# The first head's weights loaded and split ahead of the last modulation columns, the first group's features scaled as they are split, and weights in memory by tile

## The chip, the cores and the metric

The kernel runs on one core of one Trainium2 chip. The metric is the time of one execution on the device in microseconds (us), start to end; the median of several runs is used. The engines are PE (TensorE: matrix products and transposes), DVE (VectorE) and ACT (ScalarE) for the elementwise work, POOL (GpSimd) and SP (SyncE, which here only issues DMA transfers). Each engine runs its own instruction list in order and waits on semaphores for the others.

## The reference

One block of a diffusion transformer over x (2048 rows of 1024), with a context of 256 rows and a conditioning vector c. The modulation vectors come from c by a product with w_mod (1024 x 6144, six parts of 1024); the context has its own from c_ctx. Rows are normalised, scaled and shifted by two of the parts, and multiplied by w_in (1024 x 4608) for the queries, values, gates and decays of eight heads (four with learned decay, four retention heads), which run over the sequence in both directions. Then come an output product and a feed-forward part with a short convolution, w_up (1024 x 5632) and w_down.

```python
mod_x = (jax.nn.silu(c) @ w_mod[layer] + b_mod[layer])[:, None, :]
mod_c = jax.nn.silu(c_ctx) @ w_mod[layer] + b_mod[layer]
sh1, sc1, g1, sh2, sc2, g2 = jnp.split(mod_x, 6, axis=-1)
...
hx = _rmsnorm(x, norm1_g[layer]) * (1.0 + sc1) + sh1
hc = _rmsnorm(ctx, norm1_g[layer]) * (1.0 + csc1) + csh1
feats_x = _mixer_features(hx, w_in[layer], lb, (rows, cols))   # hx @ w_in, split by head
...
mix_x, _ = _bidir_mix(feats_x, ctx_states, log_gamma, ...)
x = x + g1 * (mix_x @ w_out[layer])
hx2 = _rmsnorm(x, norm2_g[layer]) * (1.0 + sc2) + sh2
x = x + g2 * _conv_ffn(hx2, w_up[layer], conv_w[layer], conv_b[layer], w_down[layer])
...
return _rmsnorm(x, final_g)
```

## The kernel before

**Tiling.** x is worked on in 4 groups of 512 rows (numbers 3, 2, 1, 0 at the start), the context as one group of 256. Large products use float16 pairs: a 32-bit tile v times a scale is kept as its rounded 16-bit value and the 16-bit rest, and a product takes three matmuls (lines 101, 102, 103). Seven products of blocks replace eight (a fast 2 x 2 scheme), so that both features and weights are kept as seven block combinations. "Splitting" means making these pairs: ACT writes the rounded value (`w[m][:, 0]`, `hx[..., 0]`), DVE the rest (`w[m][:, 1]`, `hx[..., 1]`), and DVE forms the sums and differences of blocks between.

**The start of the kernel,** which the change rewrites, consists of these chains:

- *Modulation* (`mod_loads`, `mod_first`, `mod_rows`). w_mod is loaded in column blocks of 512, named j4 = 2, 3 (the scale sc1), 0, 1 (the shift sh1), four tiles `wm` of 0.5 MB each. PE multiplies them with `silb` (silu of c) into `mod_ps`, 8 matmuls a column block (line 288); ACT copies the result to `modrow` (L254), four small matmuls turn it into columns (`modt_ps`, L259) and DVE adds the bias: `modT` (L262).
- *First rows.* The rows of group 3 (`x3`, in the buffers hc_145 to hc_151 and x_190) are loaded, squared and summed on ACT (L393), the reciprocal root comes from POOL, and ACT (L402) and DVE (L404) scale the rows.
- *First head's weights* (`head_weights(0)`). `items0` is a list of pairs (load, compute): w_z (two tiles `raw` of 0.5 MB), three further steps of its split, w_q (one tile), w_vg (two tiles, value and gate), three further steps. A compute step squares the raw tile on ACT (L738), sums over the partitions on PE (`allsum`, L124), takes a power of two as scale on DVE by five small operations (L112 to L116: `p2t`, `p2i`, `p2s`), then splits by `pair_blocks` (L691 on ACT, L692 on DVE; L748 and L749 for w_q) with the block sums on DVE (L536 to L545).
- *The feature scale* (`modulation`). From `modu` (gain times 1 + sc1) and `modT` a bound of all features is taken: `modj`, `modq`, a matmul that lays 128 partitions into a `row` (L138), a maximum (`allmax`, L140 and L142), the power of two s (`p2s`, L112 to L116), its inverse `dqx` (L366), and A = modu x s, B = modT x s (L368, L369).
- *First features* (`first_blocks`). For each pair of 128-columns kk and kk + 4, PE transposes the rows (`tp`, L411), ACT (L450) or DVE (L448) forms `ftmp` = tp x A + B, ACT casts (L429) and DVE subtracts (L430) into `hx`; afterwards eight block sums (L433, marked so in the profile) and their pairs follow. With `early=1` the two ftmp of the first column pair and its unit are formed with modu and modT as soon as these are known, and multiplied by s by DVE afterwards (L452).
- *First products.* hx times w_z (`p`), then w_q (`pa`), w_vg, with the gates (`FG`, `ct`, `cb`) between them on ACT and DVE; then the rows of group 2 (`x2`) are squared and normalised, and so on for all heads and groups.

**What sets the order.** The Python code only gives program order and buffers. `tile.TileContext(nc, schedule_with_timeline_sim=True)` makes the instruction order of each engine by a planner that simulates the program. So a small move in the code can move many rows. All loads shown go through one queue, SP's, in order. Weight tiles wait in buffers by tag ("wr" has two, "hx" seven); w_mod's first two column blocks lie in "hx", the raw tiles of w_vg in K1 and Q1.

**In memory** w_in, w_up and w_mod are kept as in the reference, rows of 4608, 5632 and 6144 numbers. A `raw` tile of 128 columns (`src[:, :, c:c + P]`) is thus read in pieces of 512 bytes, a `wm` tile in pieces of 2048 bytes.

Of the kernel before, what the change touches and what calls it, by code (L numbers as in the profile page):

```python
# [54 lines left out]
class Kern:  # L55
# [208 lines left out]
    def mod_loads(self):  # L264

        nc = self.nc
        wsrc = self.I["w_mod"][0].rearrange("(k p) n -> p k n", p=P)
        self.wm = []
        for j4, places in ((2, ("hx",) * 4), (3, ("hx",) * 4), (0, KEPT[:4]), (1, ("FG", "KTt", "ou0", "ou1"))):
            for k, tag in zip(range(0, KT, 2), places):  # L270
                w = self.slot_tile([P, 2, 512], F32, tag, "wm")
                nc.sync.dma_start(w, wsrc[:, k:k + 2, 512 * j4:512 * j4 + 512])
                self.wm += [(j4, k + i, w[:, i]) for i in range(2)]
            if j4 == 3:
                place = [h.rearrange("p k a t -> p (k a t)").bitcast(F32) for h in self.hc]
                place.append(self.slot_tile([P, G], F32, "qs", "x3"))
                self.x3 = self.load_rows(NG - 1, place)
            if j4 in (3, 1):
                self.items0[0 if j4 == 3 else 4][0]()

    def mod_first(self):

        nc = self.nc
        for j4, k, w in self.wm:
            if k == 0:
                ps = self.ps("sc", [P, 512], "mod_ps")
            q = k % 4 * B
            nc.tensor.matmul(ps[q:q + B], self.silb[:, k], w, start=k < 4, stop=k >= 4, skip_group_check=True)
            if k == KT - 1:
                if j4 == 2:  # L290
                    self.small_vectors()
                self.mod_rows(ps, 2, j4)

    def mod_later(self, j4):

        nc = self.nc
        wsrc = self.I["w_mod"][0].rearrange("(k p) n -> p k n", p=P)
        st = {}

        def item(k0):  # L300
            def load():

                st[k0] = w = [self.slot_tile([P, 512], F32, "q", "wm") for _ in range(2)]
                for kk in range(2):
                    nc.sync.dma_start(w[kk], wsrc[:, k0 + kk, 512 * j4:512 * j4 + 512])
# [108 lines left out]
    def first_blocks(self, g, xn, places, bank, early=0):  # L414
# [10 lines left out]
        def pair(m, u, v):  # L425
# [3 lines left out]
            cast = nc.scalar.copy(o[:, :, 0], v)  # L429
            self.tail = nc.vector.tensor_tensor(o[:, :, 1], v, o[:, :, 0], ALU.subtract), cast  # L430
# [4 lines left out]
        b = []  # L435
        for k0 in (0, 2):
            f = [places[k0 + r]() for r in range(2)]
            units = [(slice(k0, k0 + 2), f)] if len(f[0]) == len(f[1]) == 1 else [(slice(k0 + i, k0 + i + 1), []) for i in range(2)]
            for i in range(2):
                k = k0 + i  # L440
                at = [(v[0][:, i] if len(v) == 1 else v[i])[:, :2 * n] for v in f]
                for r in range(2):
                    kk = k + 4 * r
                    tp = self.transposed(xn, kk, bank)
                    A, B, s = self.plain if k < early else self.mod1
                    A, B = (v[:, which, kk:kk + 1] for v in (A, B))
                    if r and g in (None, NG - 1):
                        nc.vector.tensor_scalar(at[r], tp, A, B, ALU.mult, ALU.add)  # L448
                    else:
                        nc.scalar.activation(at[r], tp, AF.Identity, bias=B, scale=A)  # L450
                    if k < early:
                        nc.vector.tensor_scalar(at[r], at[r], s, None, ALU.mult)  # L452
                if len(units) == 2 or i:
# [255 lines left out]
    def head_weights(self, h):  # L709
# [317 lines left out]
    def heads(self):  # L1027
# [15 lines left out]
        for _, comp in items[4:]:  # L1043
            comp()
# [847 lines left out]
```

## Time and profile before

| | us |
|---|---|
| median of 3 runs | 2640.04 |
| lowest and highest | 2639.76 and 2642.2 |
| span of the profiled execution | 2636.4 |
| what the median has above that span | 3.6 |
| PE busy | 2515.8 (95%) |
| DVE busy | 1887.8 (72%) |
| ACT busy | 1349.2 (51%) |
| POOL busy | 425.2 (16%) |
| bytes moved by DMA | 393.97 MB, mean 149 GB/s |
| bytes moved in the first 60 us | 18.3 MB |

A row of a group reads: line, engine, operation, output <- inputs, shapes, count | busy us, mean ns of one | idle time of the engine just before and what ended it. A row of the timeline reads: start, duration, engine, line, operation, output <- inputs, and in brackets the idle time before it and what ended it. A row of the table by stretches reads: from:to, length, then busy us (and count) of PE, PEld (weight loads of PE), DVE, ACT and POOL, then PE's granted clock (1.00 is full), the share of the DMA engines and GB/s.

### The profile page before, as it was taken

The numbers are of one execution on the slowest core, as the hardware profiler recorded it, in microseconds if no ns is written. First come the engines' busy times: TensorE is split into PE (matmuls) and PEld (weight loads), VectorE is DVE, ScalarE is ACT, GpSimd is POOL, SyncE is SP. The second block draws the span as 40 slices with busy tenths as digits, with TensorE's granted clock in tenths as the row PEclk, the third lists the DMA queues.
The fourth block names the chain that finished last, engine by engine and source line by source line (L and its number), as shares of the span: only waits on it lengthen the run. The fifth ranks groups of instructions, "written<-read, shape, count | busy, mean of one in ns | idle before, by whom it ended". The sixth has DMA issues, their size and how long they took to land. (4 is left out here: it accounts for less than half of the span.)

```text
span 2636.4 us, 56190 instructions
## 1 busy us (share of the span) xinstructions
PE 2515.8 (95%) x22763; PEld 1656.9 (63%) x22763; DVE 1887.8 (72%) x4275; ACT 1349.2 (51%) x2877; POOL 425.2 (16%) x409
## 2 busy tenths in 40 slices
PE   6799998999999999988998999999999999999998
PEld 3678887889899999984454444444444444444443
DVE  4888686786878778675558778888888887323656
ACT  5886466564654454453556556565555555211220
POOL 1100000000000000000354334343434433000000
PEclk7999999999999999998999999999999999999999
DMA  8324342441548567555421332333233236544552
GB/s 295 121 95 162 124 142 85 135 152 67 177 161 291 210 210 255 189 198 192 143 81 41 116 106 99 112 107 110 101 116 120 96 113 225 206 165 159 210 206 87
DMA packets 213621, 393.97 MB, mean 149 GB/s; under 512 B 15600, under 2 KB 97748, under 8 KB 208753
## 3 DMA queue, kind: packets, MB, share of 16 engines
q1 hardware_dynamic: 203808, 373.42, 40.8%
q10 hardware_dynamic: 9248, 16.79, 1.9%
q8 instruction: 178, 2.92, 0.5%
q14 instruction: 83, 0.67, 0.1%
q0 software_dynamic: 304, 0.17, 0.0%
HBM read 298.57 MB, written 91.75 MB: 148 GB/s over the span
## 5 line engine op out<-in xcount | busy, mean ns | idle before, releaser
L101 PE MATMUL pa<-feat,w 128*128 128x512 f16 x704 | 265.0, 381 | 7.6 <-ACT ta L592 5.6
L102 PE MATMUL pa<-feat,w 128*128 128x512 f16 x704 | 267.9, 381 | 0.0
L103 PE MATMUL pa<-feat,w 128*128 128x512 f16 x704 | 267.3, 380 | 0.0
L102 PE MATMUL pd<-wd,actl 128*128 128x512 f16 x616 | 233.3, 379 | 0.0
L103 PE MATMUL pd<-wd,actl 128*128 128x512 f16 x616 | 233.3, 379 | 0.0
L101 PE MATMUL pd<-wd,actl 128*128 128x512 f16 x616 | 232.6, 379 | 0.0
L102 PEld LDWEIGHTS <-w 128*128 128x128 f16 x1232 | 120.9, 98 | 150.9 <-issue 13.0
L103 PEld LDWEIGHTS <-w 128*128 128x128 f16 x1232 | 121.0, 98 | 147.0 <-issue 3.2
L101 PEld LDWEIGHTS <-w 128*128 128x128 f16 x1232 | 120.9, 98 | 141.9 <-issue 3.1
L102 PEld LDWEIGHTS <-hx 128*128 128x128 f16 x1824 | 179.4, 98 | 7.7 <-issue 5.9
L1407 POOL TENSOR_TENSOR ssq<-ssq 128x1 f32<-128x1 f32 x16 | 4.7, 292 | 1102.8 <-ACT junk L1405 1102.8
L101 PEld LDWEIGHTS <-hx 128*128 128x128 f16 x1824 | 179.9, 99 | 2.2
L103 PEld LDWEIGHTS <-hx 128*128 128x128 f16 x1824 | 179.6, 99 | 0.9
L1642 ACT ACTIVATE st<-act,modT 128x512 f16<-128x512 f32 x154 | 107.4, 717 | 109.6 <-DVE act L1632 64.1
L1643 DVE SCALAR_TENSOR_TENSOR st<-act,modT,st 128x512 f16<-128x512 f32 x154 | 140.3, 946 | 29.7 <-ACT st L1642 28.8
L101 PE MATMUL pa<-w_vg,hx 128*128 128x128 f16 x800 | 141.8, 219 | 1.1 <-ACT ct L592 0.7
L102 PE MATMUL pa<-w_vg,hx 128*128 128x128 f16 x800 | 141.7, 219 | 0.0
L103 PE MATMUL pa<-w_vg,hx 128*128 128x128 f16 x800 | 141.7, 219 | 0.0
L101 PE MATMUL pc<-feat,w 128*128 128x512 f16 x352 | 134.8, 383 | 2.2 <-ACT feat L1417 1.3
L103 PE MATMUL pc<-feat,w 128*128 128x512 f16 x352 | 135.2, 384 | 0.0
L102 PE MATMUL pc<-feat,w 128*128 128x512 f16 x352 | 135.0, 383 | 0.1
L101 PE MATMUL pa<-hx,w_z 128*128 128x256 f16 x464 | 127.0, 274 | 1.6 <-DVE K L634 1.3
(552 smaller groups left out, 7357.3 us busy)
## 6 DMA issues: line engine op xcount, KB each, us to landing
hx<-hxd SPq DMA_DIRECT2D x212, 512.0 KB, 4.7
actd<-st SPq DMA_DIRECT2D x154, 256.0 KB, 2.0
actl<-actd SPq DMA_DIRECT2D x28, 1024.0 KB, 5.0
wur<-in_w_up_dram SPq DMA_DIRECT2D x44, 512.0 KB, 3.8
raw<-in_w_in_dram SPq DMA_DIRECT2D x36, 512.0 KB, 4.7
wm<-in_w_mod_dram SPq DMA_DIRECT2D x64, 256.0 KB, 3.7
hxd<-hx SPq DMA_DIRECT2D x28, 512.0 KB, 3.9
wdb<-in_w_down_dram SPq DMA_DIRECT2D x44, 256.0 KB, 3.8
```

The lines of the kernel that those rows point to most:

```text
L101: mm(ps, lhs(0), rhs(0), start=start, stop=False, skip_group_check=True)
L102: mm(ps, lhs(0), rhs(1), start=False, stop=False, skip_group_check=True)
L103: mm(ps, lhs(1), rhs(0), start=False, stop=stop, skip_group_check=True)
L1407: nc.gpsimd.tensor_tensor(ssq[:, 0:1], ssq[:, 0:1], ssq[:, 1:2], ALU.add)
L1642: nc.scalar.activation(p[:, 0], v, AF.Copy, scale=s)
L1643: nc.vector.scalar_tensor_tensor(p[:, 1], v, s, p[:, 0], ALU.mult, ALU.subtract)
```

## The change

1. *Load order.* The two raw tiles of w_z are loaded before everything but the identity; then column 2 of w_mod, the rows of group 3, column 3, then raw tiles q, v and g, then columns 0 and 1. The v and g tiles lie in "hx" buffers.
2. *Compute order in the code.* w_z is split first; column 2, the lower bounds (small vectors with an exponential), the norm of the first rows and column 3 follow; then w_q and w_vg are scaled and split; then columns 0 and 1.
3. *First group's features.* All eight ftmp of group 3 are formed with modu and modT, before s is known (six on ACT, two on DVE); the split applies s: ACT's cast gets a scale, DVE's subtraction becomes scalar_tensor_tensor (L431 after, ftmp x s - hx). The splits of the plain blocks follow after all the ftmp. A and B are still made for the other groups.
4. *Layout.* w_in, w_up and w_mod are rearranged on the host by tile, so that each partition's part of a raw or wm tile is 4096 contiguous bytes.

The number of PE matmuls and of DVE and ACT splits of weights stays the same; five DVE operations (three ftmp from tp, two scalings) leave the first group and two come in, and the line numbers in the code after are higher by 1 to 6 (L288 becomes L289, L692 becomes L698, L749 becomes L755, L430 becomes L434, L433 becomes L437, L748 becomes L754, L738 becomes L744).

```diff
     def mod_loads(self):
-        wsrc = self.I["w_mod"][0].rearrange("(k p) n -> p k n", p=P)
-        self.wm = []
+        self.items0[0][0]()
+        self.wm = {}
         for j4, places in ((2, ("hx",) * 4), (3, ("hx",) * 4), (0, KEPT[:4]), (1, ("FG", "KTt", "ou0", "ou1"))):
+            self.wm[j4] = []
             for k, tag in zip(range(0, KT, 2), places):
                 w = self.slot_tile([P, 2, 512], F32, tag, "wm")
-                nc.sync.dma_start(w, wsrc[:, k:k + 2, 512 * j4:512 * j4 + 512])
-                self.wm += [(j4, k + i, w[:, i]) for i in range(2)]
-            if j4 == 3:
+                nc.sync.dma_start(w, self.I["w_mod"][j4, :, k:k + 2])
+                self.wm[j4] += [w[:, i] for i in range(2)]
+            if j4 == 2:
                 place = [h.rearrange("p k a t -> p (k a t)").bitcast(F32) for h in self.hc]
                 place.append(self.slot_tile([P, G], F32, "qs", "x3"))
                 self.x3 = self.load_rows(NG - 1, place)
-            if j4 in (3, 1):
-                self.items0[0 if j4 == 3 else 4][0]()
-    def mod_first(self):
-        nc = self.nc
-        for j4, k, w in self.wm:
-            if k == 0:
-                ps = self.ps("sc", [P, 512], "mod_ps")
+            if j4 == 3:
+                self.items0[4][0]()
+                self.items0[5][0]()
+    def mod_first(self, j4):
+        nc = self.nc
+        ps = self.ps("sc", [P, 512], "mod_ps")
+        for k, w in enumerate(self.wm[j4]):
             q = k % 4 * B
             nc.tensor.matmul(ps[q:q + B], self.silb[:, k], w, start=k < 4, stop=k >= 4, skip_group_check=True)
-            if k == KT - 1:
-                if j4 == 2:
-                    self.small_vectors()
-                self.mod_rows(ps, 2, j4)
+        if j4 == 2:
+            self.small_vectors()
+        self.mod_rows(ps, 2, j4)
...
-    def first_blocks(self, g, xn, places, bank, early=0):
+    def first_blocks(self, g, xn, places, bank, plain=False):
...
             if X[m] is None:
                 X[m] = self.slot_tile([P, 4, 2, H], F16, "hx", "hx")
             o = X[m][:, u]
-            cast = nc.scalar.copy(o[:, :, 0], v)
-            self.tail = nc.vector.tensor_tensor(o[:, :, 1], v, o[:, :, 0], ALU.subtract), cast
+            if plain:
+                cast = nc.scalar.activation(o[:, :, 0], v, AF.Copy, scale=s)
+                self.tail = nc.vector.scalar_tensor_tensor(o[:, :, 1], v, s, o[:, :, 0], ALU.mult, ALU.subtract), cast
+            else:
+                cast = nc.scalar.copy(o[:, :, 0], v)
+                self.tail = nc.vector.tensor_tensor(o[:, :, 1], v, o[:, :, 0], ALU.subtract), cast
...
-        b = []
+        A, B, s = self.plain if plain else self.mod1
+        late, b = [], []
         for k0 in (0, 2):
             f = [places[k0 + r]() for r in range(2)]
...
                 for r in range(2):
                     kk = k + 4 * r
                     tp = self.transposed(xn, kk, bank)
-                    A, B, s = self.plain if k < early else self.mod1
-                    A, B = (v[:, which, kk:kk + 1] for v in (A, B))
-                    if r and g in (None, NG - 1):
-                        nc.vector.tensor_scalar(at[r], tp, A, B, ALU.mult, ALU.add)
+                    ka, kb = (v[:, which, kk:kk + 1] for v in (A, B))
+                    if r and (g is None or plain and i):
+                        nc.vector.tensor_scalar(at[r], tp, ka, kb, ALU.mult, ALU.add)
                     else:
-                        nc.scalar.activation(at[r], tp, AF.Identity, bias=B, scale=A)
-                    if k < early:
-                        nc.vector.tensor_scalar(at[r], at[r], s, None, ALU.mult)
+                        nc.scalar.activation(at[r], tp, AF.Identity, bias=kb, scale=ka)
                 if len(units) == 2 or i:
                     u = units[i if len(units) == 2 else 0][0]
...
                     for r in range(2):
-                        pair(r, u, both[r][:, :, :n])
+                        late.append((r, u, both[r][:, :, :n]))
+                        if not plain:
+                            pair(*late.pop())
                 yield
+        for a in sorted(late, key=lambda a: a[0]):
+            pair(*a)
         for u, (b11, b12, b21, b22) in b:
             sub(b11, b12, b11)
             pair(4, u, b11)
...
             vg = (3584 + o, 4096 + o)
             want += [("vg", "vg", vg)] if h < 2 * NH - 1 else [("v", "vg", vg[:1]), ("g", "vg", vg[1:])]
         nc = self.nc
-        src = self.I["w_in"][0].rearrange("(k p) n -> p k n", p=P)
+        src = self.I["w_in"]
         W, items = {}, []
         for nm, tag, cols in want:
             raws, st = [], {}
 
-            own = dict(q=("ou2",), vg=("K1", "Q1")) if h == 0 else {}
+            own = dict(q=("ou2",), vg=("hx", "hx")) if h == 0 else {}
             def load(cols=cols, raws=raws, tags=own.get(nm, ("wr", "wr"))):
                 for c, tag in zip(cols, tags):
                     raws.append(self.slot_tile([P, KT, P], F32, tag, "raw"))
-                    nc.sync.dma_start(raws[-1], src[:, :, c:c + P])
+                    nc.sync.dma_start(raws[-1], src[c // P])
...
         nc, pool = self.nc, self.mp
         W, items = self.W0, self.items0
-        self.mod_first()
-        items[5][0]()
+        for _, comp in items[:4]:
+            comp()
+        self.mod_first(2)
+        self.lower_bounds()
+        self.norm_rows(NG - 1, self.x3)
+        self.mod_first(3)
+        for _, comp in items[4:]:
+            comp()
+        self.mod_first(0)
+        self.mod_first(1)
         place = [self.gate_tile() for _ in range(4)]
         xc = self.load_rows(None, place)
-        self.norm_rows(NG - 1, self.x3)
-        for _, comp in items[:4]:
-            comp()
-        self.lower_bounds()
         self.mod1 = self.modulation(self.ep, pool, view(self.sv, V_N1, [[0, 2], [1, 8]]), self.modT[:, :, 8:16],
                                     self.modT[:, :, 0:8], 0, 1.3)
-        for _ in self.first_blocks(NG - 1, self.x3, self.temps(("ou0", "ou1", "K0", "Q0")), "pj", 1):
+        for _ in self.first_blocks(NG - 1, self.x3, self.temps(("K0", "ou0", "Q0", "ou1")), "pj", True):
             pass
-        for _, comp in items[4:]:
-            comp()
         for w, dq in W.values():
             nc.vector.tensor_tensor(dq, dq, self.dqx[:, 0:1], ALU.mult)
         prev, items = None, []
...
     def up_weights(self, j, ty):
         nc, kp = self.nc, self.kp
-        wup = self.I["w_up"][0].rearrange("(k p) n -> p k n", p=P)
+        wup = self.I["w_up"]
         raw = []
         for f in (j, j + NJ):
             r = self.slot_tile([P, KT, P], F32, "wr", "wur")
-            nc.sync.dma_start(r, wup[:, :, ty * FF + f * P:ty * FF + (f + 1) * P])
+            nc.sync.dma_start(r, wup[ty * NF + f])
             raw.append(r)
         yield
         W = [self.slot_tile([P, 2, 4, P], F16, "z", "w7") for _ in range(7)]
...
     order = np.arange(NIN)
     for o in range(2560, 3584, P):
         order[o:o + P] = o + HALVES
-    named["w_in"] = np.ascontiguousarray(named["w_in"][:, :, order])
+    tiles = lambda w, n: np.ascontiguousarray(w[0].reshape(KT, P, -1, n).transpose(2, 1, 0, 3))
+    named["w_in"] = tiles(named["w_in"][:, :, order], P)
+    named["w_up"] = tiles(named["w_up"], P)
+    named["w_mod"] = tiles(named["w_mod"], 4 * P)
     for name, a in named.items():
         arrays[f"in_{name}_dram"] = a
         I[name] = nc.dram_tensor(f"in_{name}_dram", a.shape, mybir.dt.from_np(a.dtype), kind="ExternalInput").ap()
```

**Where the planner puts it.** The queue of SP, from the first load: `wm` are tiles of w_mod, `raw` tiles of w_in, hc and the next x tile the rows of group 3, `gate` the context's rows. Before:

```order
L188 DMA ident<-in_ident_dram 128x128
L272 DMA wm<-in_w_mod_dram 128x2x512 x8
L378 DMA hc_145<-in_x_dram 128x512
L378 DMA hc_146<-in_x_dram 128x512
...
L378 DMA x_190<-in_x_dram 128x512
L730 DMA raw<-in_w_in_dram 128x8x128 x2
L272 DMA wm<-in_w_mod_dram 128x2x512 x8
L730 DMA raw<-in_w_in_dram 128x8x128
L378 DMA gate<-in_ctx_dram 128x512 x4
L730 DMA raw<-in_w_in_dram 128x8x128 x2
L378 DMA x_610<-in_x_dram 128x512
```

After:

```order
L188 DMA ident<-in_ident_dram 128x128
L736 DMA raw<-in_w_in_dram 128x1024 x2
L273 DMA wm<-in_w_mod_dram 128x1024 x4
L378 DMA hc_145<-in_x_dram 128x512
...
L378 DMA x_186<-in_x_dram 128x512
L273 DMA wm<-in_w_mod_dram 128x1024 x4
L736 DMA raw<-in_w_in_dram 128x1024 x3
L273 DMA wm<-in_w_mod_dram 128x1024 x8
L378 DMA gate<-in_ctx_dram 128x512 x4
L378 DMA x_608<-in_x_dram 128x512
```

The two raw tiles of w_z move past 8 wm and the rows, three raw tiles move ahead of the last 8 wm, and no raw tile is left between the context and x_608.

DVE, where s becomes known (`L366 COPY dqx`) before the change: L692 and L749 split weights, L536 to L545 are their block sums, L448 and L452 are ftmp operations.

```order
L366 COPY dqx<-p2i 128x1
L112 TENSOR_SCALAR p2t<-allsum 128x1
L692 SCALAR_TENSOR_TENSOR w_z<-raw,p2s,w_z 128x512
L545 TENSOR_TENSOR raw<-raw 128x512
L368 TENSOR_SCALAR A_409<-modu,p2s 128x16
L369 TENSOR_SCALAR B_410<-modT,p2s 128x16
L452 TENSOR_SCALAR ftmp<-ftmp,p2s 128x512
L692 SCALAR_TENSOR_TENSOR w_z<-raw,p2s,w_z 128x512
L452 TENSOR_SCALAR ftmp<-ftmp,p2s 128x512
L115 TENSOR_SCALAR p2i<-p2t 128x1
L113 TENSOR_SCALAR p2t<-p2t 128x1
L1046 TENSOR_TENSOR dq<-dq,dqx 128x1
```

The same engine after the change, where w_q and w_vg are split (L755, L698, L542 to L551), ahead of s:

```order
L755 SCALAR_TENSOR_TENSOR w_q<-raw,p2s,w_q 128x512
L698 SCALAR_TENSOR_TENSOR w_vg<-raw,p2s,w_vg 128x512 x2
L698 SCALAR_TENSOR_TENSOR w_vg<-raw,neg,w_vg 128x512
L542 TENSOR_TENSOR raw<-raw 128x512
...
L698 SCALAR_TENSOR_TENSOR w_vg<-raw,p2s,w_vg 128x512
L551 TENSOR_TENSOR raw<-raw 128x512
L698 SCALAR_TENSOR_TENSOR w_vg<-raw,p2s,w_vg 128x512
L262 TENSOR_TENSOR modT<-modt_ps,sv 128x4x2
L698 SCALAR_TENSOR_TENSOR w_vg<-raw,p2s,w_vg 128x512 x2
L236 TENSOR_TENSOR tmp<-sv 128x8
```

All of w_q's and w_vg's split but two operations now stands ahead of `modT` of column 0, and all of it ahead of the lower bounds (L236 on) and of what leads to s.

PE before, from column 0's `modt_ps` to the row and maximum that give s (L288 the modulation product, L411 transposes, L124 sums over squares of weights):

```order
L259 MATMUL modt_ps<-sel,modrow 128x2 x4
L288 MATMUL mod_ps<-wm,silb 32x512 x8
L411 MATMUL tp<-ident,hc_146 128x128
L411 MATMUL tp<-ident,hc_148 128x128
L411 MATMUL tp<-ident,hc_150 128x128
L411 MATMUL tp<-ident,x_190 128x128
L259 MATMUL modt_ps<-sel,modrow 128x2 x4
L124 MATMUL allsum<-ssqw,ones 128x1 x2
...
L138 MATMUL row<-ident,modq 1x128
L142 MATMUL allmax<-allmax,ones 128x1
```

PE after, the same place:

```order
L259 MATMUL modt_ps<-sel,modrow 128x2 x4
L289 MATMUL mod_ps<-wm,silb 32x512 x6
L411 MATMUL tp<-ident,hc_146 128x128
...
L411 MATMUL tp<-ident,x_186 128x128
L289 MATMUL mod_ps<-wm,silb 32x512 x2
L411 MATMUL tp<-ident,hc_145 128x128
...
L411 MATMUL tp<-ident,x_186 128x128
L138 MATMUL row<-ident,modq 1x128
L142 MATMUL allmax<-allmax,ones 128x1
```

A group of transposes (hc_146 to x_186) now stands ahead of the last two modulation matmuls of column 1, and all other groups stand ahead of `row`; the sums over the weights' squares stand earlier now. From about 130 us of the profile before on, the order of every engine is the same in both kernels.

More of the change, by code (lines that the diff above doesn't have):

```diff
@@ L277, in mod_loads @@
                 self.x3 = self.load_rows(NG - 1, place)
-            if j4 in (3, 1):
-                self.items0[0 if j4 == 3 else 4][0]()
-    def mod_first(self):
+            if j4 == 3:
+                self.items0[4][0]()
+                self.items0[5][0]()
+    def mod_first(self, j4):
         nc = self.nc
-        for j4, k, w in self.wm:
-            if k == 0:
-                ps = self.ps("sc", [P, 512], "mod_ps")
+        ps = self.ps("sc", [P, 512], "mod_ps")
+        for k, w in enumerate(self.wm[j4]):
             q = k % 4 * B
             nc.tensor.matmul(ps[q:q + B], self.silb[:, k], w, start=k < 4, stop=k >= 4, skip_group_check=True)
-            if k == KT - 1:
-                if j4 == 2:
-                    self.small_vectors()
-                self.mod_rows(ps, 2, j4)
+        if j4 == 2:
+            self.small_vectors()
+        self.mod_rows(ps, 2, j4)
     def mod_later(self, j4):
         nc = self.nc
-        wsrc = self.I["w_mod"][0].rearrange("(k p) n -> p k n", p=P)
+        wsrc = self.I["w_mod"][j4]
         st = {}
@@ L304, in load @@
                 for kk in range(2):
-                    nc.sync.dma_start(w[kk], wsrc[:, k0 + kk, 512 * j4:512 * j4 + 512])
+                    nc.sync.dma_start(w[kk], wsrc[:, k0 + kk])
             def comp():
```

## The prediction

> **What bounds the kernel now.** I read the page's busy shares and its chain first.
>
> ```profile
> span 2636.4 us, 56190 instructions
> ...
> PE 2515.8 (95%) x22763; PEld 1656.9 (63%) x22763; DVE 1887.8 (72%) x4275; ACT 1349.2 (51%) x2877; POOL 425.2 (16%) x409
> ...
> PE 40%; DVE 2%; issue 1%; ACT 0%; POOL 0%; DMA 0%; DVEq 0%; ACTq 0%; POOLq 0%; SPq 0%
> ```
>
> PE is busy for 95% of the span, so over most of it only PE's own work counts, and the change leaves that as it is. The change acts at the start, where PE is not the bound. The table by stretches shows it: after the time come the us covered, the busy time of PE, PEld, DVE, ACT and POOL, PE's granted clock, the DMA share and GB/s.
>
> ```profile
> 5.00:15.00 10.00, 8.58 (x30) 1.33 (x32) 0.34 (x2) 0.10 (x1) 1.23 (x3) 1.00 1.05 404
> 15.00:25.00 10.00, 3.99 (x22) 2.95 (x18) 1.97 (x11) 8.88 (x23) 2.03 (x6) 0.74 1.09 356
> 25.00:33.00 8.00, 7.05 (x28) 2.67 (x28) 1.46 (x4) 2.90 (x5) 0.00 (x0) 0.68 1.05 386
> ...
> 48.00:60.00 12.00, 6.47 (x26) 4.25 (x27) 12.00 (x34) 9.38 (x17) 0.00 (x0) 0.50 0.52 169
> 60.00:70.00 10.00, 7.99 (x41) 5.35 (x41) 10.00 (x18) 5.82 (x11) 0.00 (x0) 0.67 0.40 164
> 70.00:80.00 10.00, 7.74 (x65) 6.43 (x64) 8.32 (x16) 8.79 (x24) 0.00 (x0) 0.95 0.40 159
> 80.00:100.00 20.00, 18.32 (x251) 16.00 (x249) 15.54 (x30) 19.81 (x42) 5.18 (x12) 1.00 0.36 120
> ...
> 16.00:17.00 1.00, 0.07 (x1) 0.00 (x0) 0.55 (x3) 0.97 (x4) 0.00 (x0) 1.00 1.06 408
> 35.00:36.00 1.00, 0.99 (x12) 0.08 (x4) 0.00 (x0) 0.00 (x0) 0.00 (x0) 1.00 1.15 312
> ```
>
> Three limits follow each other: the DMA queue until the last modulation weights are in; DVE, with no idle time from 48 to 70 us; ACT, full from 80 to 100. The timeline gives the points between (start, duration, what the engine idled for):
>
> ```profile
> 34.06 1.92 PE L288 MATMUL mod_ps<-wm,silb 128*32 128x512 f32 x16
> ...
> 36.70 0.58 ACT L254 COPY modrow<-mod_ps 128x512 f32<-128x512 f32 x1
> ...
> 39.55 0.16 DVE L262 TENSOR_TENSOR modT<-modt_ps,sv 128x8 f32<-128x8 f32 x1
> ...
> 42.43 0.28 DVE L140 TENSOR_REDUCE allmax<-row 1x1 f32<-1x128 f32 x1 [0.78 <-PE row L138]
> ...
> 43.96 0.14 DVE L112 TENSOR_SCALAR p2t<-allmax 128x1 int32<-128x1 int32 x1
> ...
> 46.99 0.14 DVE L366 COPY dqx<-p2i 128x1 f32<-128x1 f32 x1
> ...
> 53.14 0.37 PE L101 MATMUL p<-hx,w_z 128*128 128x256 f16 x1 [0.21 <-ACT ftmp L450]
> ...
> 72.26 0.62 ACT L393 ACTIVATE junk<-x 128x512 f16<-128x512 f32 x1
> ...
> 73.49 0.68 DVE L430 TENSOR_TENSOR hx<-ftmp,hx 128x512 f16<-128x512 f32 x1
> ...
> 75.15 0.27 PE L101 MATMUL pa<-hx,w_q 128*128 128x256 f16 x1 [2.09 <-DVE ct L573]
> ```
>
> The last modulation weights arrive at about 34.5, the scale s of the features is known at 47.0, and the first group's last feature is written at 74.2. Those 27 us are DVE's: besides the features it splits w_z, w_q and w_vg. Behind that ACT squares the next rows (from 72.26) and is full. The instruction order of before and after is the same on every engine from about 130 us, so what is gained or lost by then stays to the end.
>
> **The prices.** Mean ns is the second number behind the bar; a row with x2 shows the pitch of two in a row.
>
> ```profile
> L288 PE MATMUL mod_ps<-wm,silb 128*32 128x512 f32 x64 | 15.4, 720 | 1.5 <-DMA wm<-in_w_mod_dram 1.1 <-DVE silb L208 0.5
> ...
> L692 DVE SCALAR_TENSOR_TENSOR w_vg<-raw,p2s,w_vg 128x512 f16<-128x512 f32 x6 | 4.4, 742 | 0.0
> L430 DVE TENSOR_TENSOR hx<-ftmp,hx 128x512 f16<-128x512 f32 x14 | 9.3, 682 | 0.0
> L433 DVE TENSOR_TENSOR ftmp<-ftmp 128x512 f32<-128x512 f32 x8 | 5.5, 682 | 0.0
> L448 DVE TENSOR_SCALAR ftmp<-tp,A,B 128x512 f32<-128x512 f32 x3 | 2.4, 802 | 0.0
> ...
> 42.64 1.39 DVE L692 SCALAR_TENSOR_TENSOR w_z<-raw,p2s,w_z 128x512 f16<-128x512 f32 x2
> 66.74 1.28 DVE L430 TENSOR_TENSOR hx<-ftmp,hx 128x512 f16<-128x512 f32 x2
> ...
> 24.79 1.95 ACT L402 ACTIVATE hc<-hc,rs_y 128x512 f32<-128x512 f32 x3
> 26.64 0.70 ACT L402 ACTIVATE x<-x,rs_y 128x512 f32<-128x512 f32 x1
> ...
> 37.29 1.28 ACT L239 ACT_TABLE_LOAD   x1
> ...
> 43.35 1.04 ACT L738 ACTIVATE w_vg<-raw 128x1024 f16<-128x1024 f32 x1
> 44.29 0.19 ACT L738 ACTIVATION_READ_ACCUMULATOR w_vg<-raw 128x1 f32 x1
> ...
> 50.84 1.88 PE L411 MATMUL tp<-ident,hc 128*128 128x128 f32 x7
> ```
>
> In a run of its own kind a scalar_tensor_tensor costs DVE 0.66 (1.39 less 0.74) and a tensor_tensor 0.60.
>
> **DMA queue.** The two w_z tiles (1.05 MB) go first and three more weight tiles (1.57 MB) go ahead of the last eight modulation loads, which is what SP is moved past. A tile of 0.52 MB takes 1.35 us at 388 GB/s and took about 1.8 at the 292 to 312 that the queue shows while rows of 512 bytes are read (35 to 36 us). By bytes x3 and columns 2 and 3 are in at 22.7, q, v and g by 26.8 (three times 1.35), columns 0 and 1 by 26.8 + 4.19 MB / 388 = 37.6: 3 us later than 34.5. This late end costs nothing if s waits for something else, which it does, as follows. The Trainium skill ("DMA: Bandwidth & Descriptors", Specifications) puts line rate at 512 bytes or more, by which the tile layout would bring nothing; the 312 against 408 GB/s above disagree, and by the page the forecast would be about 1 us later (2634).
>
> **The w_q and w_vg split now stands ahead of s.** ACT scales x3 after the w_z split, which shares ACT with the squares; I put its end at 28.5 (27.3 before). Then the copy of column 3 (0.58) and three squares of 1.04 + 0.19: 32.8; the sum on PE and five small DVE operations, about 1.5: p2s of g at 34.3. DVE then runs 9 scalar_tensor_tensor and 4 tensor_tensor, 9 x 0.66 + 4 x 0.60 = 8.3 us, to 42.6 (by means 9.4). In DVE's order modT of column 0 stands two from their end, at about 41.3. Behind it wait ACT's first ftmp (0.78), a group of transposes that takes over that ftmp's bank (about 0.6), and, behind those in PE's order, the last two matmuls of column 1, though their weights came at 37.6. Their copy ends at about 44.0 instead of 37.3: the split is paid here, nearly 7 us.
>
> From there to s: a table load and the exponential (1.5), four small operations of lower_bounds and modT (0.16 each as in the row of 39.55, 0.2 with the step to the next: 1.0), modj, ftmp 0.80 and two reductions (1.3) make 47.8; meanwhile ACT has another ftmp, the second table load (1.28) and two ftmp, to 49.4; eight transposes at the half clock (1.88 above for seven) come ahead of row in PE's order: 51.0; row, reduce, allmax (1.5) and five small operations without a split between them (about 0.9; before they took from 44.0 to 47.0): s at 53.2, against 47.0. Bounds: 51.2 if the x3 norm and the copies wait for nothing (2 us of my walk), 55.7 if the split goes by means (1.1) and PE stays at half clock through the group before (1.4). I take 53.2; the row nearest to it, 42.43 for allmax, only says that everything here moves with the copy.
>
> **Behind s** DVE loses the rest of the splits (4 of w_z, 2 of w_q, 7 and 4 of w_vg) and five ftmp operations, about 17 us of the 27. What is left to the last feature: five small operations (0.6), 14 pair subtractions now as scalar_tensor_tensor (14 x 0.66 = 9.2; the scale costs 14 x 0.06 = 0.8 more than before) and 8 sums (8 x 0.60 = 4.8): 14.6, to 67.8, against 74.2. **Gain 6.3 us.** By the bounds: 51.2 + 14.6 = 65.8 (8.4 gained) and 55.7 + 0.6 + 14 x 0.742 + 8 x 0.682 = 72.1 (2.0 gained). ACT's 14 casts with a scale, at the 0.70 of the row of L402, are 9.8 and hide beside DVE's 14.0; ACT also loses w_q and w_vg casts, the last two of which stand among the squares of x2 before, so the squares start right behind the last cast, at about 67 instead of 72.3. ACT is full from there to 100, so the stage moves by 5 to 7 us. The extra table load ahead of silb (1.28) is hidden: the modulation matmuls wait for w_mod's bytes until then. POOL and its queue issue what they did.
>
> **Tile layout afterwards.** The w_in and w_up loads of later heads and of the feed-forward get shorter by about 0.45 us each.
>
> ```profile
> wur<-in_w_up_dram SPq DMA_DIRECT2D x44, 512.0 KB, 3.8
> ...
> ACT w L1528 <- DMA wur<-in_w_up_dram: 34.1, 33, 4.1
> PE col L1533 <- ACT w L1528: 4.5, 2, 2.6
> ```
>
> ACT waits 34.1 us for them, but PE sees it in two waits, 4.5 us together. Two waits by 0.45 make 0.9; the ends are 0 and 3. I take 0.9.
>
> **Sum.** 6.3 + 0.9 = 7.2 less. The profiled span of 2636.4 lies 3.6 under the median of 2640.04; that remainder is start and end outside the span and I keep it: 2640.0 - 7.2 = 2632.8, rounded 2633. A difference under 0.2%, 5.3 us, is about what a measurement of this kernel can't tell from none.
>
> **Rivals.**
> - *The split is hidden after all.* If p2s of g comes by 29, DVE reaches modT of column 0 as it arrives, only the 3 us of the queue remain, s is at 50, features end at 64.6: 9.6 + 0.9 gained, 2629.5. For it: g's bytes come at 26.8. Against: column 3's copy and four scalings stand ahead of the squares on ACT. 0.14.
> - *PE paces the z products.* They are 84 matmuls, and at half clock their pitch is 0.21:
>
> ```profile
> 54.35 0.42 PE L101 MATMUL p<-hx,w_z 128*128 128x256 f16 x1
> 54.56 0.42 PE L102 MATMUL p<-hx,w_z 128*128 128x256 f16 x1
> ```
>
> From 54.2 they would last to 71.8, w_q would start near 72.3 instead of 75.15, and 2.9 + 0.9 would be gained: 2636.2. For it: the clock was 0.50 from 41 to 60. Against: PE's feed was broken there, and clock 0.67 follows at 60 to 70 as it improves. The Trainium skill ("TensorE: Matmul & The Clock Gate", Part 1) says that one busy window of about 3.4 us opens the gate, by which a PE fed without breaks runs at full speed from about 60 and this rival falls. With the cases in which s is 2 or 3 us later than I put it: 0.28, giving 2635 to 2640.
> - *Slower: the weights' squares come late.* If column 3's copy waits for its matmuls at half clock and the squares start 6 us later, p2s of g comes after 40, s after 59 and the last feature after 74.2; every us beyond is lost to the end. At p2s = 43 it is 2 to 3 us, at 48, 8 us: 2640 to 2648. For it: ACT runs in order, and column 3 lands 2.7 us later than before. Against: all four columns took PE 15.4 us before (row of L288), 3.9 each, partly at the half clock, and by the bytes column 3's can start at 17. 0.06.
>
> **Chances.** Forecast (gain 5.3 to 9.5) 0.52, hidden split 0.14, small gain 0.28, slower 0.06. Faster by over 0.2%: 0.52 + 0.12 = 0.64; within 0.2%: 0.30; slower: 0.06. The range runs from 8.4 + 3 gained, rounded to 2628, to a gain of 1 us, 2639: it leaves out half of the slower and of the no-change tail and a little of the first rival, under 0.2.
>
> **What would show it.** In the profile after: w_z split done by about 20; nine scalar_tensor_tensor on DVE between 34 and 43; the fourth modrow copy at 43 to 44; dqx at 53 (51 to 56); the first w_z product at about 54; the last feature of group 3 at 68; x2's first square at 67; the DMA queue at 380 GB/s or more also in the weight tiles; from 130 us on every instruction about 6 us earlier. Wrong would be: dqx at 50 or below (first rival), features done by 68 but w_q only at 72 (second), p2s of g after 40 (third), or a shift at 130 us that differs from that at 68, for which ACT's full stretch would be the place.

## The result, and the profile after

The changed kernel takes 2626.32 us (2626.05 to 2627.71, 4 runs), the kernel before in the same set 2640.54 (2639.76 to 2642.2, 4 runs): 14.2 us less. The ratio of the two is 0.9944, with an interval of 0.9933 to 0.9956, which is 14.8 us less (11.6 to 17.7). The forecast was 2633, from 2628 to 2639: the direction held, but the gain is twice the one forecast and the time lies outside the range.

The page after: the profiled span is 10.5 us shorter, PE's busy time the same within 3 us, and the same bytes go in a third fewer packets (213621 before):

```profile
span 2625.9 us, 56197 instructions
...
PE 2518.5 (96%) x22763; PEld 1660.3 (63%) x22763; DVE 1888.7 (72%) x4271; ACT 1353.7 (52%) x2880; POOL 425.6 (16%) x409
...
DMA packets 139892, 393.97 MB, mean 150 GB/s; under 512 B 15599, under 2 KB 15827, under 8 KB 135024
```

The same table by stretches (us covered, busy time of PE, PEld, DVE, ACT, POOL, PE's granted clock, DMA share, GB/s):

```profile
0.00:48.00 48.00, 31.94 (x132) 15.98 (x133) 24.10 (x75) 32.81 (x59) 7.25 (x21) 0.74 0.97 371
15.00:25.00 10.00, 5.39 (x20) 2.47 (x20) 4.50 (x11) 7.31 (x20) 1.85 (x6) 0.66 1.03 413
25.00:33.00 8.00, 7.25 (x34) 5.79 (x38) 3.28 (x19) 6.45 (x12) 0.17 (x1) 0.62 1.03 417
48.00:60.00 12.00, 6.80 (x29) 4.37 (x28) 8.18 (x24) 8.38 (x14) 0.00 (x0) 0.50 0.13 54
48.00:70.00 22.00, 15.76 (x87) 11.08 (x86) 17.52 (x39) 15.33 (x29) 0.00 (x0) 0.63 0.33 133
...
70.00:80.00 10.00, 9.69 (x105) 8.93 (x105) 4.66 (x13) 9.84 (x27) 2.73 (x8) 1.00 0.19 78
80.00:100.00 20.00, 17.27 (x270) 14.93 (x268) 18.68 (x36) 20.00 (x43) 1.46 (x5) 1.00 0.53 186
```

The same for the kernel before, up to 48 and from 48 to 70 us:

```profile
0.00:48.00 48.00, 28.62 (x133) 13.20 (x133) 12.98 (x58) 24.75 (x47) 7.27 (x21) 0.81 0.99 339
...
48.00:70.00 22.00, 14.46 (x66) 9.61 (x67) 22.00 (x50) 15.20 (x27) 0.00 (x0) 0.58 0.47 167
```

By 70 us DVE has done 24.10 + 17.52 = 41.62 us of work against 34.98, ACT 48.14 against 39.95. That is 6.6 us of DVE's and 8.2 of ACT's work moved into time in which they stood idle before. PE's stretch from 70 to 80 rises from 7.74 to 9.69.

The timeline after, at the points that the prediction named:

```profile
33.21 0.15 DVE L116 TENSOR_SCALAR p2s<-p2i 128x1 int32<-128x1 int32 x1
...
40.95 0.17 DVE L262 TENSOR_TENSOR modT<-modt_ps,sv 128x8 f32<-128x8 f32 x1
...
44.60 0.59 ACT L254 COPY modrow<-mod_ps 128x512 f32<-128x512 f32 x1 [2.01 <-PE mod_ps L289]
...
54.12 0.14 DVE L366 COPY dqx<-p2i 128x1 f32<-128x1 f32 x1
...
67.39 0.62 ACT L393 ACTIVATE junk<-x 128x512 f16<-128x512 f32 x1
...
70.31 0.27 PE L101 MATMUL pa<-hx,w_q 128*128 128x256 f16 x1 [0.51 <-DVE ct L579]
```

s is late by 7.1 us (54.12 against 46.99), where the forecast had 6.2; x2's first square is 4.9 us earlier (72.26 before), the first w_q product 4.8 (75.15 before). At 140 us, where both kernels run the same order, the changed kernel is 4.1 us ahead. The same products of a later step, before and then after:

```profile
139.39 0.44 PE L883 MATMUL sc<-Q,Kl 128*32 128x32 f32 x26
```

```profile
135.26 0.44 PE L889 MATMUL sc<-Q,Kl 128*32 128x32 f32 x26
```

So the start gives 4 to 5 us of the profile's 10.5. The rest comes behind 140 us, where of the change only the layout of the weights is left.

### The profile page after: what moved, and what is told of

Read it like the earlier page. It is cut to its first block, busy times and chain, and to the rows that moved or that the text cites. A ratio compares the mean times of both kernels' runs of the same rounds, so it can differ in the third digit from the quotient of the medians.

```text
span 2625.9 us, 56197 instructions
## 1 busy us (share of the span) xinstructions
PE 2518.5 (96%) x22763; PEld 1660.3 (63%) x22763; DVE 1888.7 (72%) x4271; ACT 1353.7 (52%) x2880; POOL 425.6 (16%) x409
```

## Experiments

Each kernel ran in turn with the kernel before on the same chip. Medians of one kernel differ by up to 3.5 us between sets, so the ratios to the kernel before of the same set are compared.

**The two halves apart.** e1_layout_all is the kernel before with the three weights in memory by tile; every engine's instructions stand in the old order.

```
+    tiles = lambda w, n: np.ascontiguousarray(w[0].reshape(KT, P, -1, n).transpose(2, 1, 0, 3))
+    named["w_in"] = tiles(named["w_in"][:, :, order], P)     # w_up and w_mod likewise
-    nc.sync.dma_start(raws[-1], src[:, :, c:c + P])
+    nc.sync.dma_start(raws[-1], src[c // P])
```

> The kernel before with w_in, w_up and w_mod in memory by tile and nothing else; the instruction order of every engine stays that of before. Theory A (the term for the tile layout was too small: later heads wait visibly for their weight tiles, and the trace after shows PE's lead over before grow by 1.4, 0.85, 1.2 and 1.2 us at four places where weights are summed): 6 to 9 us faster than before, 2631 to 2634. Theory B (the layout is worth what the forecast said, 1 to 2 us with the start, and the missing gain lies in the order of the start or in where PE's clock windows fall): 2638 to 2640.

Measured: 2631.88, ratio 0.9973 (0.9964 to 0.9982): 7.1 us less, from 4.7 to 9.5, as theory A had it. e2_order_only is the changed kernel with those lines as before.

> The changed kernel with the three weights in memory as before; the instruction order of every engine stays that of the changed kernel. Theory A: the start is worth the 4 to 6 us that PE's lead shows at 140 us, less what slower w_z, q, v and g loads cost there (0 to 1): 2634 to 2637. Theory B: nearly all of the gain is here, 2627 to 2630.

Measured: 2633.18, ratio 0.9975 (0.9962 to 0.9988): 6.6 us less, from 3.2 to 10, a little more than theory A had. The two sum to 13.7, against 14.8 for the whole change: two gains that add up within the intervals, half of it from the layout.

The layout's gain does not come at the start. In e1 the first square of x2 stands later than before (72.26):

```profile
73.23 0.63 ACT L392 ACTIVATE junk<-x 128x512 f16<-128x512 f32 x1
```

At 140 us the products shown above start at 141.71 in e1, 2.3 us behind the kernel before, and at the end of the profile e1 is 6.9 ahead. So the layout gains 9.2 us behind 140 us in this profile, in the later heads and the feed-forward. (e2's profile, in the old layout, is 2.9 ahead at 140 us and 2.3 at the end.) The same matmul, a sum over the squares of a later head's weights, before and then in e1:

```profile
1043.80 0.27 PE L124 MATMUL allsum<-ssqw,ones 128*128 128x1 f32 x1 [1.81 <-ACT w_g L738]
```

```profile
1039.36 0.38 PE L124 MATMUL allsum<-ssqw,ones 128*128 128x1 f32 x2 [0.56 <-ACT w_g L737]
```

PE idles 1.81 us for that weight tile before and 0.56 in e1, which by then is 4.4 us ahead. The waits of PE and ACT on weights, first before, then e1 (us, times, longest):

```profile
PE allsum L124 <- ACT w_vg L738: 2.7, 3, 1.6
PE allsum L124 <- ACT w_g L738: 1.8, 1, 1.8
...
ACT w_z L738 <- DMA raw<-in_w_in_dram: 17.7, 10, 3.2
```

```profile
ACT w L1527 <- DMA wur<-in_w_up_dram: 30.9, 31, 5.4
...
PE col L1532 <- ACT w L1527: 3.2, 2, 2.7
PE allsum L124 <- ACT w_vg L737: 1.6, 3, 0.7
PE allsum L124 <- ACT w_g L737: 0.6, 1, 0.6
...
ACT w_z L737 <- DMA raw<-in_w_in_dram: 13.9, 8, 3.1
```

With the 4.5 of PE's col that the prediction quotes, PE's waits for weight tiles go from 9.0 to 5.4: 3.6 of those 9.2 us. All of PE's waits behind 140 us together fall from 69.5 to 61.1, so nearly the whole gain is PE waiting less. The other waits that shrink stand behind values that ACT and DVE make, and some of them shrink in e2 as well, where the layout is old (ACT's V, 4.0 before, is 2.9 in e1 and 3.0 in e2); what the layout has to do with each of them stays open. A w_in tile lands 0.5 us sooner, as forecast, and a w_up tile 0.2 (median us from issue to landing; 3.8 for wur and 4.7 for raw before):

```profile
wur<-in_w_up_dram SPq DMA_DIRECT2D x44, 512.0 KB, 3.6
raw<-in_w_in_dram SPq DMA_DIRECT2D x36, 512.0 KB, 4.2
```

**Which weight's layout.** e3_layout_win keeps of e1 only w_in by tile, e4_layout_wup only w_up (`src[c // P]` alone; `wup[ty * NF + f]` alone).

> The kernel before with w_in alone in memory by tile. Theory A: the three jumps in the heads (3.4 us together) and about 1 us at the start: 4 to 5 us faster, 2635 to 2637. Theory B: 0 to 1 us, 2639 to 2640.

> The kernel before with w_up alone in memory by tile. Theory A: 1 to 3 us faster (one jump of 1.2 us at the first column sum of the feed-forward part, 1460 us, and the two waits of PE that the forecast counted): 2637 to 2639. Theory B: under 1 us. If this alone gives over 4 us, waits of ACT for w_up that PE does not show as its own idle time count too.

Measured: w_in 0.9983 (0.9973 to 0.9993), 4.5 us less; w_up 0.9988 (0.9978 to 0.9999), 3.2 less. Together 7.7, about e1's 7.1, which leaves nothing measurable for w_mod. The forecast had priced the w_up part alone.

**Which part of the order.** e5_plain_only is the kernel before with the features scaled as they are split, and nothing else:

```
-    for _ in self.first_blocks(NG - 1, self.x3, self.temps(("ou0", "ou1", "K0", "Q0")), "pj", 1):
+    for _ in self.first_blocks(NG - 1, self.x3, self.temps(("ou0", "ou1", "K0", "Q0")), "pj", True):
```

(with the new first_blocks). e6_split_only is the changed kernel with the old first_blocks.

> The kernel before with only the first group's features changed: all eight ftmp with modu and modT before s is known, the scale applied as they are split; loads, weight splits and memory layout as before. Theory A (the operations that DVE has behind s set the end of the first features): three ftmp of 0.80 and two scalings of 0.48 leave the stretch behind s, 14 subtractions become 0.06 dearer, two ftmp come in ahead of s: 1 to 3 us faster, 2636 to 2638, and the last feature of group 3 about 2 us earlier than 74.2. Theory B (these operations fall into gaps; the weights' early split is the whole gain of the start): within 1 us of before.

> The changed kernel with the first group's features as before the change (A and B with the scale, two scalings afterwards); loads, early splits and tile layout as changed. Theory A: loses 1 to 3 us against the changed kernel, 2627 to 2630, with the last feature at 71 to 72. Theory B: the same as the changed kernel within 1 us, 2625 to 2627.

Measured: e5 0.9998 (0.9988 to 1.0007), no change; e6 0.9938 (0.9926 to 0.9950), 16.4 us less, the same as the whole change within the intervals. e5's timeline:

```profile
45.86 0.59 PE L138 MATMUL row<-ident,modq 128*1 128x128 f32 x2
...
53.37 0.74 DVE L698 SCALAR_TENSOR_TENSOR w_z<-raw,p2s,w_z 128x512 f16<-128x512 f32 x1
54.02 0.14 DVE L366 COPY dqx<-p2i 128x1 f32<-128x1 f32 x1
...
71.98 1.40 DVE L431 SCALAR_TENSOR_TENSOR hx<-ftmp,p2s,hx 128x512 f16<-128x512 f32 x2
```

s is 7 us late here too, with the split of w_q and w_vg behind it. Row, which stands at 41.81 before, waits for more transposes and ftmp operations. From the maximum behind row (47.73) to s, DVE then works on eight operations of w_z's split, of which the last is shown; before it was six. The last feature is done 0.8 us sooner than before (73.38 against 74.17). e6's:

```profile
50.19 0.14 DVE L366 COPY dqx<-p2i 128x1 f32<-128x1 f32 x1
...
65.59 1.88 DVE L430 TENSOR_TENSOR hx<-ftmp,hx 128x512 f16<-128x512 f32 x3
```

The old features are done at 67.47 (65.59 + 1.88), 1.7 us before the changed kernel's, where theory A had 71 to 72; the kernel is not measurably faster than the changed one. So the order's gain comes from the early load and split of the weights; the scaled features bring nothing that these runs can measure.

**The split ahead of s or behind it.** e7_split_behind_s leaves the early loads but moves the work on w_q and w_vg behind the modulation:

```
-        for _, comp in items[4:]:
-            comp()
...
         self.mod1 = self.modulation(...)
+        for _, comp in items[4:]:
+            comp()
```

> The changed kernel with w_q and w_vg squared and split only after the modulation in the code: DVE has modT of column 0 as it arrives, so dqx should come at 46 to 49 instead of 54. Theory A (the forecast's sum: DVE's and ACT's work behind s counts as much as the time of s): the last feature is earlier by 0 to 4 us, but the split of w_vg stands behind it and among ACT's squares of x2: within 2 us of the changed kernel, 2625 to 2628. Theory C (the time of s decides and the split ahead of it is the loss): 4 to 6 us faster than the changed kernel, 2620 to 2622.

Measured: 2621.69, ratio 0.9935 (0.9922 to 0.9948), 17.2 us less. That looked better than the changed kernel, so both went again, in one set:

> The changed kernel itself once more, beside the three others of this set, as their common measure: 2624 to 2628, 13 to 15 us faster than before. A second profile of it also tells how far one execution's lead over before differs from another's (10.4 us in the first pair of profiles, 14.2 by the runs).

> The kernel with w_q and w_vg split behind s once more, beside the changed kernel. Theory A (work moved, not the time of s, is what counts): 1 to 3 us faster than the changed kernel. Theory E (the two are equal and the 4 us between their medians were the chip of the day): within 1 us.

Measured: the changed kernel 2622.86, ratio 0.9937 (0.9924 to 0.9950); the variant 2622.56, 0.9937 (0.9924 to 0.9951). No difference is measured; one of 3 us would lie within the intervals. (One profiled execution of each has spans of 2622.4 and 2618.8.) In the variant s comes 6.3 us earlier than in the changed kernel's first profile:

```profile
47.80 0.14 DVE L366 COPY dqx<-p2i 128x1 f32<-128x1 f32 x1
...
65.21 1.40 DVE L431 SCALAR_TENSOR_TENSOR hx<-ftmp,p2s,hx 128x512 f16<-128x512 f32 x2
```

and DVE is full behind it:

```profile
0.00:48.00 48.00, 29.00 (x145) 15.34 (x146) 17.12 (x62) 30.11 (x55) 7.29 (x21) 0.84 0.97 371
48.00:60.00 12.00, 7.64 (x37) 4.83 (x38) 12.00 (x34) 8.68 (x15) 0.00 (x0) 0.63 0.37 153
```

From 48 to 60 the changed kernel has DVE idle for 3.8 of 12 us while it waits for s; the variant was idle earlier, with 17.12 us of work by 48 instead of 24.10. The last feature is done at 66.61, only 2.6 us before the changed kernel's 69.17, and by 100 us both have done the same: DVE 65.04 and 64.96 us of work, ACT 78.08 and 77.98. So 6 us of s are not 6 us of the kernel. Nor does the split of w_q and w_vg have to stand ahead of s: what this variant shares with the changed kernel is the load order and the early split of w_z.

**ACT's full stretch.** After 80 us ACT was busy for 20.00 of 20 us. e8_ctx_early norms the context rows as soon as they are loaded, which takes ACT's work out of there:

```
+        xc = self.norm_rows(None, xc)
-                for _ in self.first_blocks(None, self.norm_rows(None, xc), ...
+                for _ in self.first_blocks(None, xc, ...
```

> The changed kernel with the context's rows squared and scaled right after their load in the code: four squares (0.75 each) and two scalings (0.7) leave ACT's stretch from 74 to 100 us, where the trace after shows it busy for 20.00 of 20 us, and go to the gaps between 42 and 54. Theory A (ACT's full stretch sets when the rest begins): 2 to 4 us faster than the changed kernel, 2622 to 2624, with dqx up to 1.5 us later. Theory D (PE or the clock paces that stretch; ACT only looks full): the same, 2625 to 2628.

Measured: 2626.16, ratio 0.9950 (0.9938 to 0.9962), no gain on the changed kernel. Its two stretches after 70:

```profile
70.00:80.00 10.00, 9.49 (x99) 8.56 (x98) 4.94 (x13) 7.53 (x20) 1.99 (x6) 1.00 0.30 121
80.00:100.00 20.00, 18.04 (x282) 16.19 (x281) 18.08 (x34) 19.13 (x40) 0.00 (x0) 1.00 0.58 206
```

ACT's busy time there falls by 3.2 us (29.84 to 26.66) and no gain comes of it. That speaks against theory A, but it does not settle it: from 80 to 100 us ACT is still busy for 19.13 of 20.

**DVE relieved by POOL.** POOL is idle from 48 to 70 us. Here it takes the eight feature sums, in the variant of e7 and in that of e6:

```
-        sub = lambda o, x, y: nc.vector.tensor_tensor(o, x, y, ALU.subtract)
+        sub = lambda o, x, y: (nc.gpsimd if g == NG - 1 else nc.vector).tensor_tensor(o, x, y, ALU.subtract)
```

> The same, and the eight block sums of the first group's features on POOL instead of DVE (POOL is idle there). Theory F (DVE, full from s to the last feature, still sets the pace): 8 sums of 0.6 leave it, the last feature is 3 to 4 us earlier than in the kernel without, and the time 2 to 4 us less. Theory G (POOL takes 1.3 to 1.7 us for such a sum by the rows of w_up's sums, and the casts wait for it): within 1 us.

> The changed kernel with the first group's features as before the change and their eight block sums on POOL. Theory F: 2 to 4 us faster than the same with the sums on DVE (2623.6), 2620 to 2622, last feature at 64 to 66 instead of 67.5. Theory G: 2623 to 2625.

Measured: e11 0.9968 (0.9955 to 0.9981), e12 0.9950 (0.9938 to 0.9962). e11 is 8.6 us slower than e10 of its set (2631.16 against 2622.56), which none of the theories allowed for; e12, 2627.02, looks some 3 us slower than e6, which the intervals don't tell apart, and its last feature comes at 70.8, where theory F had 64 to 66. e10's row first, then e11's:

```profile
L431 DVE SCALAR_TENSOR_TENSOR hx<-ftmp,p2s,hx 128x512 f16<-128x512 f32 x14 | 9.9, 743 | 0.0
```

```profile
L431 DVE SCALAR_TENSOR_TENSOR hx<-ftmp,p2s,hx 128x512 f16<-128x512 f32 x14 | 13.8, 1019 | 0.0
```

```profile
50.06 1.69 DVE L431 SCALAR_TENSOR_TENSOR hx<-ftmp,p2s,hx 128x512 f16<-128x512 f32 x1
...
56.17 0.74 DVE L755 SCALAR_TENSOR_TENSOR w_q<-raw,p2s,w_q 128x512 f16<-128x512 f32 x1
```

```profile
L437 POOL TENSOR_TENSOR ftmp<-ftmp x8: 1618/1714/1787, 49.4 to 63.4; 128x512 f32<-128x512 f32 x8
```

A split of DVE's that begins in the middle of one of POOL's sums takes 1.69 to 1.75, and between 56.2 and 58.2, when POOL pauses, 0.74 again. DVE is spared eight sums of 0.68, 5.4 us, and pays back 3.9 in these 14 operations, 1.0 in two of w_q's split (1.246 each on average) and 2.0 in four of w_vg's (1.233): more than it was spared. The sums themselves last 13.4 us on POOL, and ACT's last cast waits 0.95 for one. The last feature comes at 70.2 instead of 66.6.

## Why the prediction was wrong, point by point

**The step that failed is "Tile layout afterwards".** It was put at 0.9 us with ends of 0 and 3, and e1 measured 7.1 (4.7 to 9.5). By the profiles, the changed kernel gains 6.4 us behind 140 us (4.1 ahead there, 10.5 at the end) and 8.6 in a second profile (e9; 5.4 and 14.0). The price of a tile was near for w_in (0.45 us forecast, 0.5 in the landing rows), but for w_up, where it was used, it is 0.2. Wrong was the count of places: the step looked at w_up and its two waits of PE only. PE's waits in the sum over the squares of later heads' weights, 2.7 and 1.8 us, stood in the same view of waits as the quoted row of col and were not counted; nor were ACT's waits for w_in (33.0 us in all before, 27.5 in e1). Nor is a wait shortened by one tile's price: the wait for w_g shown above fell by 1.25 us, the two of col by 1.3 together. With 7.1 for 0.9 the forecast's sum would have been 6.3 + 7.1 = 13.4, against 14.2 measured.

**The start came near its forecast, perhaps 1 to 3 us short of it.** The forecast was 6.3 us. e2's runs give 6.6, with a wide interval (3.2 to 10); in the changed kernel's profile the last feature is 5.0 us earlier and the lead at 140 us is 4.1 (5.4 in e9, 2.9 in e2), where the forecast had about 6 for every instruction from 130 us on. The walk, forecast and then trace: p2s of g 34.3 and 33.21; modT of column 0 41.3 and 40.95; the split's end 42.6 and 42.43; s 53.2 and 54.12; last feature 67.8 and 69.17; first square of x2 67 and 67.39. The fourth modrow copy ends at 45.19 (44.60 + 0.59), 1.2 later than put, and s is 0.9 late by it.

**The reason given is borne out in part.** The walk put the gain at the end of the first features: s later, but so much less work behind it that the last feature, and with it the w_q products and all that follows, come earlier. The table sets these two points of each kernel's profile (us earlier than before) beside the ratios from above, with the matmuls that PE has done by 100 us.

| kernel | last feature done | first w_q product | PE matmuls by 100 us | ratio |
|---|---|---|---|---|
| before | 0 | 0 | 510 | 1 |
| e5_plain_only (old layout) | 0.8 | 0.8 | 532 | 0.9998 |
| e2_order_only (old layout) | 4.8 | 3.2 | 584 | 0.9975 |
| e11_behind_s_pool | 3.9 | 2.7 | 535 | 0.9968 |
| e12_old_features_pool | 3.4 | 4.9 | 569 | 0.9950 |
| e8_ctx_early | 4.0 | 3.8 | 588 | 0.9950 |
| changed, first profile | 5.0 | 4.8 | 588 | 0.9944 |
| e9, the changed kernel again | 4.1 | 3.9 | 588 | 0.9937 |
| e6_split_only | 6.7 | 7.0 | 590 | 0.9938 |
| e10_behind_s_again | 7.6 | 6.5 | 589 | 0.9937 |

The kernels that start the w_q products 3.2 to 7.0 us earlier have 569 to 590 matmuls done by 100 us and are the ones that gain. e5 starts them 0.8 earlier and gains nothing; e11, which POOL holds back, starts them 2.7 earlier and keeps little beside the 7 us of the layout. This agrees with the reason given, but it does not prove it: a difference of 3 us between two ratios can't be told from none, so whether the 1.7 us of e6's last feature or the 2.6 of e10's reach the end stays open. The time of s alone is shown not to decide: in e5 it is 7 us later and the last feature 0.8 earlier. Nor does the amount of DVE's work that is moved ahead of 70 us: it is 6.6 us in the changed kernel and 3.8 in e10, with no difference measured between the two.

**The queue** moved 413 and 417 GB/s from 15 to 33 us, where 356 and 386 stood and 388 was forecast. **ACT, full from 80 to 100, as what hands the start on** was not confirmed by e8, and not ruled out either.

**The rivals.** The hidden split had the total nearest to the result (2629.5) but not its sign: s at 54, not 50. PE did not pace the z products: the first w_q product starts at 70.31, not 72.3, and 1.1 us behind the last feature (in e2, though, at 71.91, 2.5 behind it). The slower rival needed p2s of g past 40; it was 33.21.

**The remainder of 3.6 us outside the span** was 1.8 in the changed kernel's profiled execution (2627.71 less 2625.9). The 3.6 set the median of three executions against the span of one.

## What to carry to other kernels

Price a faster transfer by every wait for what it feeds, on every line of the kernel: list all of PE's waits whose releaser is work on loaded tiles, not only those of the line at hand. Ask of a start when the products that fill PE can begin; the time of one landmark on the way (here s, 6 us earlier or later) can be worth much less than its own shift. An idle engine is no free help if its operations slow the engine that it helps.

## What the runs showed of the hardware

**Rows of 512 bytes are slow to load.** In the start, where the queue is never empty, one us of reading w_in took 290 to 312 GB/s before (312 in the prediction's row of 35 to 36 us). The same weights by tile, with 4 KB in a row, after; by the queue's order and bytes the queue reads q, v and g of w_in here:

```profile
24.00:25.00 1.00, 0.00 (x0) 0.00 (x0) 0.00 (x0) 0.00 (x0) 0.67 (x5) 1.00 1.03 422
```

By the Trainium skill ("DMA: Bandwidth & Descriptors", Specifications) 512 bytes are enough for line rate. The layout alone brought 7.1 us in 2640 here, so the measurement decides against it.

**POOL and DVE hinder each other.** Beside POOL's sums single scalar_tensor_tensor operations of DVE took 1.69 to 1.75 us instead of 0.74 (1.019 on average over the 14). POOL's sum of 128x512 f32 took 1.71 there; the fastest of its kind in the kernel before took 1.27, and on DVE it takes 0.68. The Trainium skill ("SBUF — State Buffer", SBUF: two separate sides) says that a DVE operation with two SBUF inputs and a GpSimd operation that reads SBUF take a shared pair of ports in turn, the one blocking the other; e11's rows agree.

**Two executions of one kernel differ by 3.5 us.** The changed kernel's two profiled spans are 2625.9 and 2622.4 (e9), so by the one the gain is 10.5 us and by the other 14.0. At 140 us e9 is already 1.3 us ahead (134.01 against 135.26 for the products shown above). Two stretches further on, after first and then e9:

```profile
250.00:275.00 25.00, 21.41 (x349) 18.57 (x336) 18.87 (x37) 14.88 (x34) 0.00 (x0) 0.86 0.40 127
440.00:460.00 20.00, 13.87 (x144) 12.05 (x142) 10.71 (x45) 13.48 (x30) 0.00 (x0) 0.83 0.01 2
```

```profile
250.00:275.00 25.00, 22.27 (x366) 19.66 (x364) 19.53 (x43) 14.77 (x34) 0.00 (x0) 0.93 0.45 140
440.00:460.00 20.00, 14.10 (x145) 12.60 (x145) 12.22 (x52) 10.63 (x26) 0.00 (x0) 0.91 0.00 1
```

In the first profile the granted clock is lower by 0.07 over 25 us and by 0.08 over 20, an estimated 1.75 + 1.6 = 3.35 us of PE time at full clock. That is not the whole account: from 1160 to 1300 us it is e9 that has the lower clock (0.92 against 0.95), and over the whole span both have the same, 0.980 and 0.979. So the clock was lowered at different places in two executions of one program. A gain of a few us is not to be read from one pair of spans.
